# MLA's values of two head groups from seven products of two k-tiles, ahead of the second group's queries

## Chip, cores and metric

The kernel runs on one core of one Trainium2 chip. The time is device microseconds of one execution; before the change the median of three runs is 2367.46 us. One execution was also taken by the profiler, and all rows come from it.

## What is computed

A trunk of two residual layers over 256 positions with a width of 2048, in float32. Layer 0 runs 32 Mamba-2 heads and 16 heads of multi-head latent attention (MLA) behind one input projection, and joins both in one output projection; layer 1 is stick-breaking attention; a SwiGLU network follows each. The change concerns MLA alone:

```python
def mla_mixer(c_q, c_kv, k_rope, q_norm, kv_norm, w_uq, w_ukv, cos, sin):
    q = (rms_norm(c_q, q_norm) @ w_uq).reshape(bsz, seq, MLA_HEADS, MLA_NOPE + MLA_ROPE)
    kv = (rms_norm(c_kv, kv_norm) @ w_ukv).reshape(bsz, seq, MLA_HEADS, MLA_NOPE + MLA_V)
    q_nope, q_pe = jnp.split(q, [MLA_NOPE], axis=-1)
    k_nope, v = jnp.split(kv, [MLA_NOPE], axis=-1)
    ...
        s = (jnp.einsum('bqhd,bkhd->bhqk', q_nope[:, q0:q1], k_nope[:, :q1])
             + jnp.einsum('bqhr,bkr->bhqk', q_pe[:, q0:q1], k_pe[:, :q1])).astype(jnp.float32) * scale
        ...
        outs.append(jnp.einsum('bhqk,bkhd->bqhd', p.astype(v.dtype), v[:, :q1]))
```

The values v of a head are 128 columns of `w_ukv` times the 512 normalised latent columns of c_kv: four k-tiles of 128 rows, for two token tiles of 128.

## The kernel before

**Split products.** Every float32 operand is split in a high part, made by a cast on ACT (`split`, L346), and a low part, the difference, made by a subtract on DVE (L352). A product of one k-tile is three matmuls: high by high, low by high, high by low. The low part of a weight overwrites its raw tile.

**Weights.** SP loads weights into six raw slots of 128x2048, in the order in which the code asks for them and as slots come free. High parts lie in four buffers in this stage. A copy that frees a PSUM bank is marked `urgent`; `after_urgent` lets a weight's cast be issued only behind the urgent copies of four weights earlier.

**PSUM.** Four accumulator banks, taken in rotation from `self.banks` by `acc`. Score blocks, transposes and P.V products use another pool.

**Order.** PE's order is that of the code. ACT, DVE, SP and POOL each run one queue in an order set when the program is built, by priorities: weights first in the order of their use, urgent work ahead of it.

**The MLA stage** (`mla_group`, L1464) handles four groups of four heads, one after the other:

- the rope part of the queries, `project` with 256 columns (matmuls L460, L462, L463), copied by ACT (L1502), turned by POOL;
- the queries without rope and the keys, `project_T` (L508 and L510, copy L517);
- the values, `project` with 512 columns: 4 k-tiles x 2 token tiles x 3 = 24 matmuls, copied out by ACT (L407);
- four heads, spawned at the end of the group as tasks (`mla_head`, L1516) that wake 2, 6, 10 and 14 ticks later, and so run among the next group's projections: a score block on PE (L1526 to L1528), its row maximum on DVE (L1533, L1534), the exp on ACT in two halves (L1536), the normalising on DVE (L1538, L1540); seven ticks later three transposes (L1544) and a copy (L1546), four ticks later the product with the values (L1550, L1551).

Behind group 3 comes the output projection (`project_residual`, in the order `LATE`). It makes two blocks of 512 columns at a time from seven products (`pair`, matmuls L794) whose weight operands are sums made on DVE (L741), and whose data operands are sums too (L691, L701). ACT copies a product out of its bank where it is needed twice (L815), and DVE adds it to another (a "take", L643). The first such pair starts with the products M1 and M5. The heads of group 3 run inside it.

Of the kernel before, what the change touches and what calls it, by code (L numbers as in the profile page):

```python
# [47 lines left out]
class Trunk:  # L48
# [526 lines left out]
    def more_sums(self, st):  # L575

        sub = lambda o, p, q: self.nc.vector.tensor_tensor(o, p, q, op=ALU.subtract)
        add = lambda o, p, q: self.nc.vector.tensor_tensor(o, p, q, op=ALU.add)
        yield 40
        self.join(st["xT"][2][0])  # L580
        a = {}
        for j, (hi, lo) in enumerate(st["xT"][2][1]):
            r = self.s2([2, S])
            add(r, hi.bitcast(F32), lo.bitcast(F32))
            a.update({(t, j): r[:, :, t * P:(t + 1) * P] for t in range(2)})
        yield 1
        s12, s34 = self.s2([4, P]), self.s2([4, P])
        s1, s2, s3, s4 = s12[:, :2], s12[:, 2:], s34[:, :2], s34[:, 2:]
        add(s1, a[1, 0], a[1, 1])
        sub(s2, s1, a[0, 0])  # L590
        sub(s3, a[0, 0], a[1, 0])
        sub(s4, a[0, 1], s2)
        for s in (s12, s34):
            yield 1
            hi, lo = self.s2([4, P], F32R), self.s2([4, P], F32R)
            self.split(hi, lo, s)
            st["N"].append((hi, lo))

    def norm_operand(self, st, j, g):
# [567 lines left out]
    def even(self, st):  # L1167
        nc, i = self.nc, self.i
        win = i["w_in"][0]
        xT = self.pairs(st["xT"], True)  # L1170
        xdt = [[self.spare[2 * n + t] for t in range(2)] for n in range(4)]
        y = [[self.s2([512]) for _ in range(2)] for _ in range(4)]
        conv, ssd = {}, []
        for n in (4, 5, 0, 1, 2, 3):
            ps = self.project(xT, self.cols(win, OFF_XBC + n * 512, first=n == 4), KD)
# [3 lines left out]
            raw = self.evac(ps, AF.Copy, rstd, self.twins)  # L1179
# [8 lines left out]
        cT = []  # L1188
        for off, g in ((OFF_CQ, self.g_q), (OFF_CKV, self.g_kv)):
            ps = self.project(xT, self.cols(win, off), KD)  # L1190
            raw = self.evac(ps, AF.Copy, rstd, self.twins)
            ssq = self.small([P, 2], "ssqc")
            with self.urgent():
# [3 lines left out]
                r = self.rstd(ssq, 512)  # L1197
# [7 lines left out]
        for n in range(4):  # L1205
            ps = self.project(xT, self.cols(win, OFF_Z + n * 512), KD)
# [6 lines left out]
            src, g = lambda t, k: self.twins[t].words[:, k * P:(k + 1) * P], self.g_ssd[:, 4 * n:4 * n + 4]  # L1213
# [24 lines left out]
        self.slots["wh"] += self.more_high  # L1238
        self.project_residual(uT, lambda n: self.cols(wo, n * 512), scale)
        oT = self.operand()  # L1240
        for g in range(4):
            self.mla_group(g, self.pairs(cT[:1]), self.pairs(cT[1:]), oT)
        st = self.norm_begin()
        self.project_residual(oT, lambda n: self.cols(wo, n * 512, r0=SSD_W), None,
                              lambda n: self.norm_next(st, n, self.g_ffn[0]), ("M5", "M3"), self.LATE)
# [218 lines left out]
    def mla_group(self, g, cq, ckv, oT):  # L1464
# [5 lines left out]
        def heads(wd, c0, n):  # L1470
            def view(w, k0, k1):
                for k in range(k0, k1):
                    yield (w[:, k - k0, :4 * n].rearrange("p (h c) -> p h c", c=n),
                           wd[:, k, h0:h0 + 4, c0:c0 + n])
            return view

        qp = self.evac_rope(self.project(cq, heads(wuq, 128, 64), 4, 256), self.twins[g % 2])
# [127 lines left out]
```

## Time and profile before

| | |
|---|---|
| median of the runs | 2367.46 us (2367.45 to 2368.05) |
| the profiled execution, its own time | 2367.47 us |
| its span | 2365.8 us |
| granted TensorE clock, mean | 0.999 |
| group 0's values and group 1 | 415.78 to 448.95 us |
| group 2 | 448.95 to 479.27 us |
| group 3 | 479.27 to 509.60 us |
| first products of the output projection | from 509.60 us |

The span runs from the first to the last instruction; 1.7 us of the execution lie around it. A row of the timeline gives the start of an instruction, its length, engine, line and operation, the tiles written and read with their shapes, and in brackets the idle time ahead of it with what ended it. "x4" joins several like instructions. Lengths of neighbours on an engine overlap a little, so the step from start to start is the cost of one in a row. A matmul's length is far longer than that step, because several are in flight.

### The profile page before, as it was taken

The page shows a single profiled execution, that of the slowest core. Times are in us where ns is not written, and L with a number is a line of the kernel's source. Part 1 is how long each engine was busy: PE and PEld are TensorE (multiplying, and loading weights), DVE is VectorE, ACT ScalarE, POOL GpSimd, SP SyncE. Part 2 cuts the span into 40 slices and gives each one's busy share as a digit, 9 for nine tenths or more (in the row PEclk, how much of TensorE's full clock was granted, in tenths as well). Part 3 has the DMA queues.
Part 4 walks back from the last instruction along what each step waited for, and adds up shares of the span by engine and source line. Part 5 has one row for each costly group of instructions (what it writes and reads, how often), then busy time and mean ns, then how long its engine had stood idle before and what let it go on. Part 6 is the DMA issues. An engine that isn't in the chain of part 4 may idle for free.

```text
span 2365.8 us, 28204 instructions
## 1 busy us (share of the span) xinstructions
PE 2350.3 (99%) x11088; PEld 1955.3 (83%) x11088; DVE 1986.8 (84%) x1639; ACT 1461.5 (62%) x1478; POOL 213.1 (9%) x273
## 2 busy tenths in 40 slices
PE   9999999999999999999999999999999999999998
PEld 7888888988888888888888888888888888888886
DVE  6776587589998889989887898889997988899884
ACT  6655565566665655566655786776665666555663
POOL 1342001110000000000000020110000000000011
PEclk9999999999999999999999999999999999999999
DMA  8655556445666767776776655556657777777773
GB/s 274 205 194 177 184 196 189 133 142 195 230 204 206 226 217 216 221 221 220 219 238 210 202 183 176 186 174 239 229 200 212 222 223 224 216 215 226 218 252 109
DMA packets 271428, 486.33 MB, mean 206 GB/s; under 512 B 22268, under 2 KB 47488, under 8 KB 271296
## 3 DMA queue, kind: packets, MB, share of 16 engines
q1 hardware_dynamic: 255200, 445.95, 57.4%
q0 software_dynamic: 15232, 37.01, 6.4%
q8 instruction: 87, 1.43, 0.2%
q10 hardware_dynamic: 864, 1.57, 0.2%
q14 instruction: 45, 0.37, 0.0%
HBM read 459.24 MB, written 25.20 MB: 205 GB/s over the span
## 4 chain that ended last, share of the span: by engine, by line
PE 95%; DVE 2%; ACT 2%; issue 1%; DMA 0%; SPq 0%; ACTq 0%; DVEq 0%
PE acc L794 54%; PE acc L460 11%; PE acc L463 11%; PE acc L462 11%; PE tr L357 1%; PE acc L508 1%; ACT wh L346 1%; PE at L1455 1%; PE acc L510 0%; DVE wsum L741 0%; DVE wsum L352 0%; DVE w L352 0%; PE at L1526 0%; DMA xres<-in_x_dram 0%; PE at L1527 0%
## 5 line engine op out<-in xcount | busy, mean ns | idle before, releaser
L352 DVE TENSOR_TENSOR w<-w,wh 128x2048 fp32r<-128x2048 f32 (+2 forms) x399 | 892.9, 2245 | 189.7 <-ACT wh L346 183.1
L794 PE MATMUL acc<-wh,s 128*128 128x512 f32 x3896 | 985.4, 391 | 1.5 <-ACT s L815 1.2
L346 ACT CAST wh<-w 128x2048 fp32r<-128x2048 f32 (+2 forms) x399 | 744.7, 1874 | 340.3 <-PE acc L463 147.0
L794 PEld LDWEIGHTS acc<-wh,s 128*128 128x128 f32 x3896 | 725.5, 188 | 150.9 <-ACT s L815 1.7
L460 PE MATMUL acc<-wh,s 128*128 128x512 f32 (+1 forms) x1216 | 482.0, 396 | 0.1
L463 PE MATMUL acc<-wh,s 128*128 128x512 f32 (+1 forms) x1216 | 471.0, 387 | 0.1
L462 PE MATMUL acc<-w,s 128*128 128x512 f32 (+1 forms) x1152 | 445.4, 387 | 0.0
L794 PE MATMUL acc<-w,s 128*128 128x512 f32 x1312 | 355.6, 389 | 0.2 <-DVE w L352 0.2
L794 PEld LDWEIGHTS acc<-w,s 128*128 128x128 f32 x1312 | 246.2, 188 | 52.1 <-DVE w L352 0.6
L463 PEld LDWEIGHTS acc<-wh,s 128*128 128x128 f32 x1216 | 228.3, 188 | 47.9 <-DVE s L381 0.6
L460 PEld LDWEIGHTS acc<-wh,s 128*128 128x128 f32 x1216 | 228.5, 188 | 45.3 <-issue 1.7
L462 PEld LDWEIGHTS acc<-w,s 128*128 128x128 f32 x1152 | 216.7, 188 | 41.8 <-issue 1.4
L352 DVE TENSOR_TENSOR wsum<-wsum,wh 128x2048 fp32r<-128x2048 f32 (+1 forms) x101 | 217.8, 2156 | 3.7 <-ACT wh L346 3.7
L346 ACT CAST wh<-wsum 128x2048 fp32r<-128x2048 f32 (+1 forms) x101 | 182.9, 1811 | 53.9 <-PE acc L794 35.7
L956 POOL DMA_DIRECT2D saved<-s x64 | 55.9, 995 | 1107.1 <-ACT s L955 1106.0
L346 ACT CAST wh<-lent 128x2048 fp32r<-128x2048 f32 (+1 forms) x62 | 114.6, 1859 | 62.0 <-DMA lent<-in_w_gate_dram 19.9
L352 DVE TENSOR_TENSOR lent<-lent,wh 128x2048 fp32r<-128x2048 f32 (+1 forms) x62 | 137.1, 2216 | 11.6 <-ACT wh L346 11.2
L741 DVE TENSOR_TENSOR wsum<-w,wsum 128x2048 f32<-128x2048 f32 (+1 forms) x52 | 104.2, 2004 | 17.8 <-PE acc L794 15.9
L794 PE MATMUL acc<-wsum,s 128*128 128x512 f32 x380 | 104.6, 390 | 1.4 <-DVE wsum L352 1.4
L794 PEld LDWEIGHTS acc<-wsum,s 128*128 128x128 f32 x380 | 71.2, 188 | 17.1 <-DVE wsum L352 2.2
L815 ACT COPY s<-acc 128x512 f32<-128x512 f32 x88 | 51.6, 588 | 39.1 <-PE acc L794 39.1
L741 DVE TENSOR_TENSOR wsum<-w,w 128x2048 f32<-128x2048 f32 (+1 forms) x35 | 71.3, 2038 | 1.7 <-DMA w<-in_w_qkv_dram 1.7
(268 smaller groups left out, 1888.8 us busy)
## 6 DMA issues: line engine op xcount, KB each, us to landing
w<-in_w_down_dram SPq DMA_DIRECT2D x80, 1024.0 KB, 5.0
w<-in_w_gate_dram SPq DMA_DIRECT2D x76, 1024.0 KB, 5.1
w<-in_w_up_dram SPq DMA_DIRECT2D x76, 1024.0 KB, 5.1
w<-in_w_qkv_dram SPq DMA_DIRECT2D x48, 1024.0 KB, 5.0
w<-in_w_in_dram SPq DMA_DIRECT2D x45, 1024.0 KB, 5.2
w<-in_w_out_even_dram SPq DMA_DIRECT2D x32, 1024.0 KB, 5.0
saved<-s POOLq DMA_DIRECT2D x64, 256.0 KB, 7.2
w<-in_w_out_odd_dram SPq DMA_DIRECT2D x16, 1024.0 KB, 4.9
```

The lines of the kernel that those rows point to most:

```text
L346: cast = nc.scalar.copy(hi, src).ins
L352: return nc.vector.tensor_tensor(lo, src, hi.bitcast(F32), op=ALU.subtract).ins
L357: self.nc.tensor.transpose(out.bitcast(F32R), src, self.ident_r)
L460: nc.tensor.matmul(ps[t], hi[:, ts], wh, start=k == 0, stop=False)
L462: slot.used(nc.tensor.matmul(ps[t], hi[:, ts], wl, start=False, stop=False), self.clock)
L463: nc.tensor.matmul(ps[t], lo[:, ts], wh, start=False, stop=k == nk - 1)
L508: nc.tensor.matmul(ps[:, h % 2], wh[:, hs], x, start=k == n == 0, stop=False)
L741: ins = self.nc.vector.tensor_tensor(half(o, so), half(p, sp), half(q, sq), op=ALU.subtract).ins
L794: m = nc.tensor.matmul(ps[b], x, y, start=b not in started, stop=stop, skip_group_check=True)
L815: copied = nc.scalar.copy(o, ps[b]).ins
L956: nc.gpsimd.dma_start(self.saved[n][:, t], s, accum_op=ALU.add)
L1455: nc.tensor.matmul(py[:, ds], rows[c, h // 4][:, h % 4], xdt[c][:, ds], start=True, stop=True)
```

## The change

The values of groups g-1 and g, for g = 1 and 3, are made together by a new function `quad`, ahead of group g's queries; groups 0 and 2 have no value projection of their own. The 512 latent columns are taken as two halves of two k-tiles, the two token tiles and the two groups of heads likewise as halves, so that the product is one of 2x2 blocks by 2x2 blocks, made with seven products M1 to M7 in place of eight. Each product is 2 k-tiles x 3 = 6 matmuls of 128x512 (L641 after the change): 42 for two groups.

The products are issued in the order M1, M2, M5, M6, M3, M7, M4. M1, M6 and M7 go into the bank z, M5 and M3 into p3, M2 into p2, M4 into p4. M1, M5, M6 and M7 are copied out by ACT (L661) and four takes on DVE (L1593) add them to what ends in the banks; these are the values. Afterwards the banks stand in the order p2, p4, z, p3. The four weight sums t1 to t4 are half-width subtracts and adds on DVE; two raw slots hold loaded weights (c0, c1), two the sums (n2, n3). The data sums of the four products that need them (`quad_sums`) are made once, in a task that is spawned ahead of the first group, and serve both quads. The products wait for weights and banks as before; the tasks of heads run among them at the ticks.

```diff
+    def quad_sums(self, st, block, wait):
...
+        yield wait
+        self.join(block[0])
+        a = {}
+        for j, (hi, lo) in enumerate(block[1]):
+            r = self.s2([2, S])
+            add(r, hi.bitcast(F32), lo.bitcast(F32))
...
+        add(s1, a[1, 0], a[1, 1])
+        sub(s2, s1, a[0, 0])
+        sub(s3, a[0, 0], a[1, 0])
+        sub(s4, a[0, 1], s2)
+        for s in (s12, s34):
+            yield 1
+            hi, lo = self.s2([4, P], F32R), self.s2([4, P], F32R)
+            self.split(hi, lo, s)
+            st["N"].append((hi, lo))
+
+    ONLY = ("t1", "t2", "t4", "n0", "n2", "t3", "n1", "n3")
+
+    def quad(self, st, va, vb, left, right, nk=4, order=ONLY, tag="wsum"):
...
+        for m, v in (("c0", va), ("c1", vb)):
+            raw[m] = self.wload(v, 0)
+        self.join(st["quad"])
+        names = ("z", "p3", "p2", "p4")
+        z, p3, p2, p4 = self.banks
+        self.banks = [p2, p4, z, p3]
...
+            if keep:
+                with self.urgent():
+                    kept[keep] = self.s2([512])
+                    nc.scalar.copy(kept[keep], ps[b])
+            with self.urgent():
+                for c, q, take, t in (("p2", "M1", left, 0), ("p4", "M7", left, 1), ("z", "M5", right, 1),
+                                      ("p3", "M6", right, 0)):
+                    if todo[c] == 0 and q in kept:
+                        todo[c] = -1
+                        take(t, ps[c], kept[q])
+
+        bank = {"M1": "z", "M6": "z", "M7": "z", "M5": "p3", "M3": "p3", "M2": "p2", "M4": "p4"}
...
+            if m == "t1":
+                src["n2"] = self.wtile(tag)
+                self.wsub(src["n2"], raw["c1"], raw["c0"], 0, 0, 0)
...
+            elif m == "n0":
+                halves(self.wsplit(raw["c0"], 4, 4, sync), (0, "M1"), (1, "M2"))
+            elif m == "n2":
+                halves(self.wsplit(src["n2"], 4, 4, sync), (0, "M5"), (1, "M6"))
+            elif m == "n1":
+                halves(self.wsplit(raw["c1"], 4), (1, "M3"), (0, "M7"))
+            elif m == "n3":
+                halves(self.wsplit(src["n3"], 2, 2), (0, "M4"))
...
+        kv = {"xT": cT[1:], "N": []}
+        kv["quad"] = self.spawn(self.quad_sums(kv, cT[1], 4))
         for g in range(4):
-            self.mla_group(g, self.pairs(cT[:1]), self.pairs(cT[1:]), oT)
+            self.mla_group(g, self.pairs(cT[:1]), self.pairs(cT[1:]), kv, oT)
...
+        if g % 2 == 0:
+            self.v = [[None, None], [None, None]]
+        else:
+            def take(n):
+                def sum_up(t, c, s):
+                    nc.vector.tensor_tensor(s, c, s, op=ALU.add)
+                    self.v[n][t] = s
+                return sum_up
+            self.quad(kv, heads(wkv, 128, 128, -4), heads(wkv, 128, 128), take(0), take(1), tag="w")
+        v = self.v[g % 2]
         qp = self.evac_rope(self.project(cq, heads(wuq, 128, 64), 4, 256), self.twins[g % 2])
         q = self.project_T(cq, heads(wuq, 0, 128))
         k = self.project_T(ckv, heads(wkv, 0, 128))
-        v = self.evac(self.project(ckv, heads(wkv, 128, 128), 4))
```

The diff moves instructions on engines whose order it does not write out. The first place is ACT between group 0's keys and group 1's rope queries. Names are tile names with buffer numbers: `s2` data tiles, `wh` high parts, `w4` to `w9` raw slots, `acc` accumulators, `at` scores, `mx` and `sm` a head's maximum and sum. Before:

```order
L346 CAST wh0_65<-w8_78 128x2048
L407 COPY s2_310_3273<-acc_308_3241 128x512
L407 COPY s2_311_3275<-acc_309_3242 128x512
L346 CAST wh1_66<-w4_70 128x2048
L346 CAST wh2_67<-w5_72 128x4x256
L1536 ACT_TABLE_LOAD
L1536 ACTIVATE s2_319_3308,sm_318_3307<-at_316_3299,mx_317_3306 128x128
L1536 ACTIVATE s2_319_3308,sm_318_3307<-at_316_3299,mx_317_3306 128x256
L1502 COPY s2_320_3329<-acc_314_3279 128x256
```

The same place after the change, where `acc_318` is the bank z, `acc_319` p3, and the copies L661 are, in turn, those of M1, M5, M6 and M7:

```order
L346 CAST wh0_65<-w8_78 128x1024
L661 COPY s2_322_3284<-acc_318_3269 128x512
L346 CAST wh1_66<-w4_70 128x4x256
L1656 ACT_TABLE_LOAD
L1656 ACTIVATE s2_326_3301,sm_325_3300<-at_323_3292,mx_324_3299 128x128
L661 COPY s2_327_3319<-acc_319_3270 128x512
L661 COPY s2_328_3327<-acc_318_3269 128x512
L1656 ACTIVATE s2_326_3301,sm_325_3300<-at_323_3292,mx_324_3299 128x256
L346 CAST wh2_67<-w5_72 128x2048
L1656 ACTIVATE s2_332_3354,sm_331_3353<-at_329_3345,mx_330_3352 128x128
L661 COPY s2_333_3363<-acc_318_3269 128x512
```

Two evacuations that stood ahead of the first head's exp are gone; copies of M5 and M6 now stand between its two halves, and that of M7 between those of the second head.

The second place is DVE ahead of the output projection's first pair. `wsum` and some `w` tiles take the weight sums. Before, from the first of the sums on:

```order
L741 TENSOR_TENSOR wsum10_82<-w9_80,w7_76 128x2048
L1534 TENSOR_SCALAR mx_409_3948<-mx_409_3948 128x2
L352 TENSOR_TENSOR w7_75<-w7_76,wh2_67 128x2048
L1538 RECIPROCAL sm_410_3949<-sm_410_3949 128x2
L1540 TENSOR_SCALAR s2_411_3950<-s2_411_3950,sm_410_3949 128x128
L1540 TENSOR_SCALAR s2_411_3950<-s2_411_3950,sm_410_3949 128x256
L741 TENSOR_TENSOR wsum11_84<-w8_78,wsum10_82 128x2048
```

After the change, from the second quad's last two takes (M7's and M4's) to the same sum and the second one:

```order
L1593 TENSOR_TENSOR s2_416_3956<-acc_400_3877,s2_416_3956 128x512
L1593 TENSOR_TENSOR s2_425_4011<-acc_403_3880,s2_425_4011 128x512
L1658 RECIPROCAL sm_423_4001<-sm_423_4001 128x2
L1660 TENSOR_SCALAR s2_424_4002<-s2_424_4002,sm_423_4001 128x128
L1660 TENSOR_SCALAR s2_424_4002<-s2_424_4002,sm_423_4001 128x256
L850 TENSOR_TENSOR wsum10_82<-w5_72,w6_74 128x2048
L352 TENSOR_TENSOR w4_69<-w4_70,wh1_66 128x2048
L1653 TENSOR_REDUCE mx_434_4073<-at_433_4066 128x1 x2
L352 TENSOR_TENSOR w6_73<-w6_74,wh2_67 128x2048
L1654 TENSOR_SCALAR mx_434_4073<-mx_434_4073 128x2
L850 TENSOR_TENSOR wsum11_84<-w9_80,wsum10_82 128x2048
```

The first weight sum of the projection stood behind group 2's values on PE and now stands behind the takes of a quad; the low part of group 3's keys (`w4`) stands behind it.

More of the change, by code (lines that the diff above doesn't have):

```diff
@@ L597, in more_sums @@
             st["N"].append((hi, lo))
+    def quad_sums(self, st, block, wait):
+        sub = lambda o, p, q: self.nc.vector.tensor_tensor(o, p, q, op=ALU.subtract)
+        add = lambda o, p, q: self.nc.vector.tensor_tensor(o, p, q, op=ALU.add)
+        yield wait
[4 more added lines that the diff above has]
+            add(r, hi.bitcast(F32), lo.bitcast(F32))
+            a.update({(t, j): r[:, :, t * P:(t + 1) * P] for t in range(2)})
+        yield 1
+        s12, s34 = self.s2([4, P]), self.s2([4, P])
+        s1, s2, s3, s4 = s12[:, :2], s12[:, 2:], s34[:, :2], s34[:, 2:]
+        add(s1, a[1, 0], a[1, 1])
[3 more added lines that the diff above has]
+        for s in (s12, s34):
+            yield 1
+            hi, lo = self.s2([4, P], F32R), self.s2([4, P], F32R)
+            self.split(hi, lo, s)
+            st["N"].append((hi, lo))
@@ new lines, with mm, add, ops @@
+    ONLY = ("t1", "t2", "t4", "n0", "n2", "t3", "n1", "n3")
+    def quad(self, st, va, vb, left, right, nk=4, order=ONLY, tag="wsum"):
+        nc, raw, src = self.nc, {}, {}
+        for m, v in (("c0", va), ("c1", vb)):
[4 more added lines that the diff above has]
+        self.banks = [p2, p4, z, p3]
+        ps = {n: self.pacc.tile([P, 512], F32, name=self.nm("acc"), tag=b, bufs=1)
+              for n, b in zip(names, (z, p3, p2, p4))}
+        more = nk // 4 - 1
+        todo = {"z": 3 + more, "p3": 2 + more, "p2": 1 + more, "p4": 1 + more}
+        started, kept = set(), {}
+        def mm(b, x, y, stop=False):
+            m = nc.tensor.matmul(ps[b], x, y, start=b not in started, stop=stop, skip_group_check=True)
+            started.add(b)
+            return m
+        def add(b, x, w, keep=None):
+            wh, wl, slot = w
+            n = len(x)
+            for k, (hi, lo) in enumerate(x):
+                mm(b, hi, wh[:, k])
+                mm(b, lo, wh[:, k])
+                if k == 1 and n > 2:
+                    self.tick()
+            for k, (hi, lo) in enumerate(x):
+                self.clock += 1
+                slot.used(mm(b, hi, wl[:, k], stop=k == n - 1), self.clock)
+            self.tick()
+            todo[b] -= 1
+            if keep:
[9 more added lines that the diff above has]
+        bank = {"M1": "z", "M6": "z", "M7": "z", "M5": "p3", "M3": "p3", "M2": "p2", "M4": "p4"}
+        def ops(m):
+            if m in ("M1", "M2", "M4"):
+                return [self.operand_tile(st, k + 2 * (m != "M1"), m == "M4") for k in range(2)]
+            n = (5, 6, 7, 3).index(int(m[1]))
+            return [tuple(o[:, n % 2 * 2 + k] for o in st["N"][n // 2]) for k in range(2)]
+        def halves(w, *ms):
+            wh, wl, slot = w
+            for n, m in ms:
+                at = slice(2 * n, 2 * n + 2)
+                add(bank[m], ops(m), (wh[:, at], wl[:, at], slot), m if m in ("M1", "M5", "M6", "M7") else None)
+        sync = mybir.DependencyClass.Sync
+        for m in order:
+            if m == "t1":
+                src["n2"] = self.wtile(tag)
+                self.wsub(src["n2"], raw["c1"], raw["c0"], 0, 0, 0)
+            elif m == "t2":
+                self.wsub(src["n2"], raw["c1"], src["n2"], 1, 1, 0)
+            elif m == "t3":
+                self.wsub(raw["c1"], raw["c1"], raw["c1"], 0, 1, 0)
+            elif m == "t4":
+                src["n3"] = self.wtile(tag)
+                self.wsub(src["n3"], raw["c0"], src["n2"], 0, 1, 1)
+            elif m == "n0":
[7 more added lines that the diff above has]
+            else:
+                k0 = 4 * int(m[1])
+                w = self.wsplit(self.wload(va if m[0] == "a" else vb, k0), 8)
+                for t, b in enumerate(("p2", "p4")) if m[0] == "a" else ((1, "z"), (0, "p3")):
+                    add(b, [self.operand_tile(st, k0 + k, t) for k in range(4)], w)
@@ L1462, in ssd_group, with mla_group @@
         nc.gpsimd.tensor_tensor(y[1], y[1], yo, op=ALU.add)
-    def mla_group(self, g, cq, ckv, oT):
+    def mla_group(self, g, cq, ckv, kv, oT):
         nc, i = self.nc, self.i
@@ L1468, in mla_group, with heads @@
         h0 = 4 * g
-        def heads(wd, c0, n):
+        def heads(wd, c0, n, more=0):
             def view(w, k0, k1):
@@ L1473, in view @@
                     yield (w[:, k - k0, :4 * n].rearrange("p (h c) -> p h c", c=n),
-                           wd[:, k, h0:h0 + 4, c0:c0 + n])
+                           wd[:, k, h0 + more:h0 + more + 4, c0:c0 + n])
             return view
+        if g % 2 == 0:
+            self.v = [[None, None], [None, None]]
+        else:
+            def take(n):
[5 more added lines that the diff above has]
+        v = self.v[g % 2]
         qp = self.evac_rope(self.project(cq, heads(wuq, 128, 64), 4, 256), self.twins[g % 2])
```

## The prediction, made before the changed kernel ran

> **What bounds the kernel now.** I read the page first: the busy times with their share of the span, and the chain that ended last.
>
> ```profile
> PE 2350.3 (99%) x11088; PEld 1955.3 (83%) x11088; DVE 1986.8 (84%) x1639; ACT 1461.5 (62%) x1478; POOL 213.1 (9%) x273
> ...
> PE 95%; DVE 2%; ACT 2%; issue 1%; DMA 0%; SPq 0%; ACTq 0%; DVEq 0%
> ```
>
> PE is busy 99% of the span and carries 95% of the chain. A whole-run share says nothing of one stage, so I cut the MLA stage by windows: group 0's values with group 1, then group 2, group 3, and the start of the output projection. The columns are the window and its length, then the busy time and count of PE, of its weight loads, of DVE, ACT and POOL, the granted clock, the DMA share and GB/s.
>
> ```profile
> 415.78:448.95 33.17, 33.17 (x224) 30.30 (x223) 17.54 (x30) 19.32 (x36) 5.36 (x12) 1.00 0.49 128
> 448.95:479.27 30.32, 30.32 (x217) 28.24 (x216) 15.12 (x30) 16.93 (x41) 5.13 (x12) 1.00 0.47 139
> 479.27:509.60 30.33, 30.33 (x218) 28.24 (x217) 24.83 (x35) 17.06 (x37) 10.45 (x12) 1.00 0.41 139
> 509.60:560.00 50.40, 49.16 (x246) 41.06 (x245) 41.53 (x56) 33.76 (x55) 0.00 (x0) 1.00 0.43 146
> ```
>
> PE has no idle time in the groups, so there a matmul less is time saved, and a wait of PE is time lost. DVE is half idle in groups 1 and 2 and fuller (24.83 of 30.33) in group 3, where the output projection is prepared. The only wait is 50.40 - 49.16 = 1.24 behind 509.60.
>
> **The saving.** The first two rows are the first and the last of group 0's 24 value matmuls, the third the first of the next rope queries.
>
> ```profile
> 415.78 0.40 PE L460 MATMUL acc<-wh,s 128*128 128x512 f32 x1
> ...
> 421.02 0.39 PE L463 MATMUL acc<-wh,s 128*128 128x512 f32 x1
> 421.25 0.28 PE L460 MATMUL acc<-wh,s 128*128 128x256 f32 x1
> ```
>
> 24 matmuls in 421.25 - 415.78 = 5.47 us: 0.228 each. Two groups take 48 before and 42 after, so both pairs of groups save 12 x 0.228 = 2.74 us. One product of six is 1.36.
>
> [...]
>
> **What the quad waits for: four banks, two of them used again.** M5 goes into the bank p3 and M3 into it again, after ACT has copied M5 out; the same holds for M1, M6 and M7 in z. ACT works in its written order, and there the copy of M5 stands behind an exp of a head whose scores PE has just made, and that exp behind DVE's maximum. The prices:
>
> ```profile
> 422.68 0.39 PE L1526 MATMUL at<-s,s 128*128 128x128 f32 x2
> ...
> 424.13 0.36 PE L460 MATMUL acc<-wh,s 128*128 128x256 f32 x1
> ```
>
> A score block between two projection matmuls is 424.13 - 422.68 = 1.45. On ACT:
>
> ```profile
> 415.98 0.59 ACT L517 COPY s<-acc 128x512 f32<-128x512 f32 x1 [2.65 <-PE acc L510]
> ...
> 426.91 1.28 ACT L1536 ACT_TABLE_LOAD   x1
> 428.21 0.37 ACT L1536 ACTIVATE s<-at,mx 128x128 f32<-128x128 f32 x1
> 428.47 0.19 ACT L1536 ACTIVATION_READ_ACCUMULATOR s<-at,mx 128x1 f32 x1
> 428.57 0.47 ACT L1536 ACTIVATE s<-at,mx 128x256 f32<-128x256 f32 x1
> ...
> 433.62 1.91 ACT L346 CAST wh<-w 128x2048 fp32r<-128x2048 f32 x1
> ```
>
> The first row began 0.20 after the matmul that it waited for (415.78, where the keys end): the handoff from PE to a reader. The first half of an exp takes 0.36 (428.21 to 428.57). On DVE:
>
> ```profile
> 387.63 0.69 DVE L643 TENSOR_TENSOR s<-acc,s 128x512 f32<-128x512 f32 x1
> ...
> 423.87 2.29 DVE L352 TENSOR_TENSOR w<-w,wh 128x2048 fp32r<-128x2048 f32 x1 [3.16 <-DMA w<-in_w_uq_dram]
> 426.07 0.61 DVE L1533 TENSOR_REDUCE mx<-at 128x1 f32<-128x128 f32 x2
> 426.72 0.17 DVE L1534 TENSOR_SCALAR mx<-mx 128x2 f32<-128x2 f32 x1
> 426.93 1.22 DVE L352 TENSOR_TENSOR w<-w,wh 128x1024 fp32r<-128x1024 f32 x1
> ```
>
> Followers start about 0.09 before the end shown (423.87 + 2.29 against 426.07), so 2.20 for a full low part; two reduces are 0.65 to the next start.
>
> *A, first quad, M3.* From the end of M2: handoff 0.20, take 0.69, n3's low part 1.22, reduces 0.65, the rope queries' low part 1.22, maximum 0.17: 4.15, less about 0.15 of overlaps, 4.0. Then the table load 1.28, the exp 0.36, the copy of M5 0.59: 6.2. PE's cover is the score block 1.45 and M5 and M6 at 1.36: 4.2. Wait **2.0**. Behind M3 on PE stand M7 and head 1's scores, so all of it is lost. If the load does not wait for the maximum but runs early, A is 0.7.
>
> [...]
>
> *D, second quad to the next rope queries.* The banks are left as p2, p4, z, p3, so the next rope queries take p2 and, three 256-column matmuls later (0.12 each, an estimate as half the 0.228 for half the width, together 0.36), p4, which M4, the last product, has just filled. It comes free with DVE's take of M4, which stands behind M7's, which needs M7's copy, behind head 2's exp, behind its maximum. From the end of that score block: 0.20 + 0.65 + 0.17 = 1.02, exp 0.36, copy 0.59, two takes 1.29, in all 3.26, and 0.06 to restart. PE has M4 1.36 and 0.36. Wait **1.6**.
>
> *B, the same place in the first quad.* The reduces stand behind the queries' low part (2.29), this behind its cast (1.91), the cast behind the exp that A delays: DVE reaches the reduces about 0.6 later. Wait **2.2**.
>
> *C, second quad, M3.* Here a second score block lies ahead of M6: 1.02 + 0.36 + 0.59 + 0.06 = 2.03 against M6's 1.36. Wait **0.6**.
>
> Each such wait is seen once today, at the output projection's third product:
>
> ```profile
> 516.71 1.07 PE L794 MATMUL acc<-wsum,s 128*128 128x512 f32 x4
> ...
> 517.86 1.10 ACT L815 COPY s<-acc 128x512 f32<-128x512 f32 x2
> ...
> 519.02 1.20 PE L794 MATMUL acc<-wh,s 128*128 128x512 f32 x4 [1.24 <-ACT s L815]
> ```
>
> PE restarts 0.06 after the copy, and the first four matmuls take 0.13 longer (1.20, 1.07): that surcharge I add per wait. This wait stays; with its products' preparation shifted I walk it at 0.9, so -0.3.
>
> **What the quad takes from the output projection (E).** Before, group 3's values lay ahead of the first pair as cover.
>
> ```profile
> 484.63 2.28 DVE L741 TENSOR_TENSOR wsum<-w,w 128x2048 f32<-128x2048 f32 x1
> ...
> 504.47 0.69 DVE L352 TENSOR_TENSOR s<-s,s 128x512 fp32r<-128x512 f32 x1 [0.31 <-ACT s L346]
> ...
> 509.60 1.07 PE L794 MATMUL acc<-wh,s 128*128 128x512 f32 x4
> ```
>
> The pair's first operand's low part was ready at 505.16 and wanted at 509.60: 4.4 us of slack; the first weight sum ran from 484.63. Now 5.47 of values are gone from group 3's stretch, and two of its four score blocks: 30.33 - 5.47 - 2 x 1.45 = 22.0, with D's 1.6 about 23.5 from M4's end to the pair. DVE, from the last take (1.9 after M4's end), has seven full-width operations, 7 x 2.20 = 15.4, and some 21 small ones (reduces, maxima, normalising, four operand sums at 0.69), 7.2, then the operand's low part 0.69: 25.2. Wait **1.7**, between 1.0 (small ones overlap) and 2.2 (an operation waits for its cast).
>
> **At nothing.** The operand sums (2 x 0.69, four half ones, two splits: about 4.3 of DVE, 1.2 of ACT) run in group 0's queries and keys, ahead of 415.78, as do the first quad's weight sums (four half-width ones): if DVE is late there, n2 starts late, 1 us for 1 us. The four copies replace four evacuations on ACT. The quad's weights lie in four of the six raw slots. A load takes
>
> ```profile
> w<-in_w_out_even_dram SPq DMA_DIRECT2D x32, 1024.0 KB, 5.0
> ```
>
> 5.0 us to land, and SP issues in the order in which slots come free, as before. The tightest is the second operand of the first weight sum: its slot is free at M7's end, a score block and M4 (1.45 + 1.36 = 2.8) ahead of M4's end, so it lands 2.2 behind it, just when DVE comes to it. POOL's rope work, 5.13 to 5.36 busy in a group of 30, isn't moved.
>
> **Sum.** 2.0 + 2.2 + 0.6 + 1.6 + 1.7 = 8.1; five surcharges 0.65; -0.3; saving -2.74: +5.7. The profiled execution took 2367.47, the median of the runs shown is 2367.46, so both give 2367.47 + 5.7 = **2373.2 us**, 0.24% slower. About 0.2%, 4.7 us, is what a measurement can tell from no change: 2362.7 to 2372.2.
>
> **Rivals.** *The cover at the pair suffices* (not slower): DVE's seven full-width operations end early, because the weight sums and low parts find the idle half of group 2's DVE time, 30.32 - 15.12, ahead of M4's end. For: loads may land early, and the small operations overlap. Against: they are ordered behind the takes. It decides where DVE's load after the last take falls under 21.6 (23.5 - 1.9, operand included) instead of 23.3. E and its surcharge go: 2373.2 - 1.8 = 2371.4. Chance 0.25.
>
> *All waits hide*: the copies are not late, since PE lags behind what my walk gives it or DVE's chain is shorter. Only the saving stands: 2364.7. For: no wait at PE in any group today. Against: A to D start at an event of PE itself (the end of M2 or of a block), so no lead of the other engines helps. Waits together must fall under 2.7 to be faster at all. Chance 0.12.
>
> *Weights late*: the six slots are held longer, and the tightest load above lands after DVE wants it, and every microsecond is added to E. A whole landing would be 5.0; I take 3: 2376.2. For: 4 of 6 slots for a block of 10 us. Against: DMA share 0.4 to 0.5. Chance 0.15.
>
> *The clock swings*: two quads of 42 x 0.228 = 9.6 us at half speed would give +19, 2392. Against: 1.00 in every row here, the one with the wait too. Chance 0.02. [...] That the change fails to do what it says is excluded by the order of PE's instructions: 42 where 48 were.
>
> **Chances.** The forecast, all five waits, 0.46, spreads over 2371 to 2375.5, four fifths of it above 2372.2: 0.37. With the late weights and the clock, 0.54 slower. No change: 0.09 of the forecast, the 0.25 of the pair's rival and about 0.09 of the hidden waits: 0.43. Faster by over 0.2% needs more than the whole saving: 0.03. Range: the low end is the four block waits at their lower ends (A 0.7, the others less by a third) without E, 2367.5; the high end the weights' rival with 0.8 more in E and A, 2377.0. It leaves out most of the hidden waits, the clock and a tail.
>
> **What would show it.** Right: PE waits of 2.0 and 0.6 at the quads' M3 ended by ACT's copy, of 2.2 and 1.6 at the rope queries' second bank ended by DVE's take, and one ahead of the first pair ended by DVE's low part of an operand; the stage's windows longer by the waits less 2.74. Wrong: a quad without idle time, a wait ended by a DMA, or a clock under 1.00.

## The result and the profile after

The changed kernel takes 2380.76 us (median of six runs, 2377.28 to 2381.4) where the kernel before takes 2367.64 (six runs, 2367.45 to 2368.05): a ratio of 1.0054 with a 95% interval of 1.0044 to 1.0064, so 13 us or 0.54% slower. The forecast was 2373.2 with a range up to 2377.0: the direction was right and the size was not.

The page after, the same two lines as before (busy times, and the chain that ended last); its span is 2379.0 us, its own time 2380.7:

```profile
PE 2352.0 (99%) x11076; PEld 1955.2 (82%) x11076; DVE 2015.8 (85%) x1667; ACT 1468.4 (62%) x1484; POOL 225.0 (9%) x273
...
PE 92%; issue 4%; DVE 2%; ACT 1%; POOL 1%; DMA 0%; SPq 0%; ACTq 0%; DVEq 0%; POOLq 0%
```

PE issues 12 instructions less and is yet busy 1.7 us longer, and POOL, which nobody asked to do more, is busy 12 us longer (213.1 before). Both are hints at the two things that the forecast missed. What PE waits for in the stage, from 380 to 560 us (line waited at, releaser, sum, times, longest):

```profile
PE tr L357 <- POOL twin L1470: 5.1, 2, 3.5
PE acc L460 <- DVE s L1593: 3.3, 2, 1.9
PE acc L641 <- ACT s L661: 2.3, 2, 1.7
PE acc L903 <- ACT s L924: 0.7, 1, 0.7
PE acc L903 <- DVE s L352: 0.5, 1, 0.5
```

The second to the fifth row are the forecast's B and D, A and C, the old wait, and E. The first, the costliest, is in no term of its sum. In the timeline, both waits for POOL and those of the first quad:

```profile
417.65 0.53 PE L357 MATMUL tr<-ident_r,twinwords 128*128 128x128 f32 x4 [3.48 <-POOL twin L1470]
...
430.01 1.20 PE L641 MATMUL acc<-wh,s 128*128 128x512 f32 x4 [1.74 <-ACT s L661]
...
438.18 0.39 PE L460 MATMUL acc<-wh,s 128*128 128x256 f32 x1 [1.86 <-DVE s L1593]
...
521.37 0.54 PE L357 MATMUL tr<-ident_r,twinwords 128*128 128x128 f32 x4 [1.66 <-POOL twin L1470]
```

The second quad's waits at the same places are 0.54 and 1.49, E is 0.48 and the old one 0.68. All eight sum to 11.9 where there was one of 1.24: 10.7 more. The same stretch by windows, cut at the first waits (the column before the DMA share is the granted clock):

```profile
414.17:417.65 3.48, 0.01 (x2) 0.00 (x1) 2.58 (x4) 2.90 (x5) 3.35 (x5) 1.00 0.02 3
418.50:421.70 3.20, 3.20 (x15) 3.02 (x14) 2.60 (x2) 0.79 (x2) 0.00 (x0) 0.54 0.00 0
436.32:438.18 1.86, 0.00 (x1) 0.00 (x1) 1.35 (x3) 1.86 (x5) 0.00 (x0) 1.00 0.92 246
438.30:441.50 3.20, 3.20 (x17) 3.20 (x18) 2.89 (x4) 2.18 (x3) 0.00 (x0) 0.54 1.09 321
```

In the second and the fourth row, behind two of the waits, PE works with no idle time at half the clock. Cut finer, each stretch is 3.41 us long (418.05 to 421.46, 438.53 to 441.94) and loses half of it, together 3.4. That is why the busy time grew with less work in it.

Put together: 10.7 of waits, 3.4 of half clock and seven restarts more at about 0.13 (0.9), less 2.74 saved, are 12.3. From the start of group 0's rope queries to the output projection's third product PE took 117.99 us before (401.03 to 519.02) and takes 131.85 now (401.06 to 532.91), 13.9 more. So 1.6 of the stage's loss is in no term: its matmuls follow each other a little less closely, and the cause is not shown. The rest of the kernel is 0.7 shorter, and the spans differ by 13.2.

Why is POOL late for the wait of 3.48? Its rope work in group 0, in the changed kernel (start and length):

```profile
404.23 0.98 POOL L1464 TENSOR_TENSOR ropea<-s,rope 128x128 f32<-128x128 f32 x1 [83.46 <-ACT s L1622]
405.17 1.44 POOL L1465 TENSOR_TENSOR ropeb<-s,rope 128x128 f32<-128x128 f32 x1
...
408.57 2.50 POOL L1469 TENSOR_TENSOR ropeb<-s,rope 128x128 f32<-128x128 f32 x1
411.03 2.51 POOL L1464 TENSOR_TENSOR ropea<-s,rope 128x128 f32<-128x128 f32 x1
...
417.14 0.46 POOL L1470 TENSOR_TENSOR twin<-ropea,ropeb 128x128 f32<-128x128 f32 x1
```

and DVE beside it:

```profile
408.21 5.00 DVE L352 TENSOR_TENSOR w<-w,wh 128x2048 fp32r<-128x2048 f32 x2
```

The two operations of 2.50 and 2.51 lie in step with DVE's two subtracts, 5.00 together. All twelve took from 404.23 to 417.60, 13.4 us, and PE's transposes start 0.05 later. The profile of before had the sign of it, and the forecast did not look there:

```profile
404.19 1.04 POOL L1353 TENSOR_TENSOR ropea<-s,rope 128x128 f32<-128x128 f32 x1 [83.48 <-ACT s L1502]
405.19 1.53 POOL L1354 TENSOR_TENSOR ropeb<-s,rope 128x128 f32<-128x128 f32 x1
406.69 0.46 POOL L1357 TENSOR_TENSOR ropea<-s,rope 128x128 f32<-128x128 f32 x1
```

The first multiply takes 1.04 beside the end of a subtract of DVE (402.62 to 404.90), the second 1.53 beside another (405.18 to 406.40), and the third, of the same shape, 0.46 once DVE is idle. In group 3 of the same profile the full price stood, on POOL and on DVE beside it:

```profile
490.34 2.50 POOL L1355 TENSOR_TENSOR twin<-ropea,ropeb 128x128 f32<-128x128 f32 x1
489.99 2.54 DVE L741 TENSOR_TENSOR wsum<-w,wsum 128x2048 f32<-128x2048 f32 x1
```

There the rope took 10.6 us already before the change (488.54 to 499.15), and PE came for it at 499.75, just late enough not to wait.

### The profile page after: what moved, and what is told of

Same layout as the page of the kernel before. It is cut to its first block, busy times and chain, and to the rows that moved or that the text cites. A ratio compares the mean times of both kernels' runs of the same rounds, so it can differ in the third digit from the quotient of the medians.

```text
span 2379.0 us, 28225 instructions
## 1 busy us (share of the span) xinstructions
PE 2352.0 (99%) x11076; PEld 1955.2 (82%) x11076; DVE 2015.8 (85%) x1667; ACT 1468.4 (62%) x1484; POOL 225.0 (9%) x273
## 4 chain that ended last, share of the span: by engine, by line
PE 92%; issue 4%; DVE 2%; ACT 1%; POOL 1%; DMA 0%; SPq 0%; ACTq 0%; DVEq 0%; POOLq 0%
PE acc L903 52%; PE acc L460 11%; PE acc L463 11%; PE acc L462 11%; PE tr L357 1%; PE acc L508 1%; PE at L1566 1%; DVE w L352 0%; PE acc L641 0%; ACT wh L346 0%; DVE wsum L850 0%; PE acc L510 0%; PE at L1646 0%; PE at L1647 0%; DMA xres<-in_x_dram 0%
## 5 line engine op out<-in xcount | busy, mean ns | idle before, releaser
L460 PE MATMUL acc<-wh,s 128*128 128x512 f32 (+1 forms) x1184 | 469.8, 397 | 3.5 <-DVE s L1593 3.3
L463 PE MATMUL acc<-wh,s 128*128 128x512 f32 (+1 forms) x1184 | 459.1, 388 | 0.1
L462 PE MATMUL acc<-w,s 128*128 128x512 f32 (+1 forms) x1120 | 433.4, 387 | 0.0
L903 PEld LDWEIGHTS acc<-w,s 128*128 128x128 f32 x1312 | 246.2, 188 | 52.1 <-DVE w L352 0.6
L462 PEld LDWEIGHTS acc<-w,s 128*128 128x128 f32 x1120 | 211.1, 189 | 41.0 <-issue 1.4
L850 DVE TENSOR_TENSOR w<-w,w 128x2048 f32<-128x2048 f32 (+1 forms) x35 | 74.1, 2117 | 0.9 <-PE acc L510 0.8
```

The costliest lines, as they stand in the source:

```text
L460: nc.tensor.matmul(ps[t], hi[:, ts], wh, start=k == 0, stop=False)
L462: slot.used(nc.tensor.matmul(ps[t], hi[:, ts], wl, start=False, stop=False), self.clock)
L463: nc.tensor.matmul(ps[t], lo[:, ts], wh, start=False, stop=k == nk - 1)
L850: ins = self.nc.vector.tensor_tensor(half(o, so), half(p, sp), half(q, sq), op=ALU.subtract).ins
L903: m = nc.tensor.matmul(ps[b], x, y, start=b not in started, stop=stop, skip_group_check=True)
```

## The experiments

The theory after reading: the five block waits are as walked; besides them DVE's new work (weight sums, operand sums) slows POOL's rope until PE waits for it, and PE's waits are followed by half clock. The rivals: POOL is slow for another reason; the clock falls for another reason, such as the load of the quad; the place ahead of group 1's queries is at fault and not the seven products. Times are medians; the kernel before took 2367.51 to 2367.56 beside these runs.

**1. Another order of banks.**

```diff
-        self.banks = [p2, p4, z, p3]
+        self.banks = [p2, p3, z, p4]
```

> The change with one line altered: after a quad the banks stand in the order p2, p3, z, p4, so the next rope queries take p2 and p3 and not the bank of the last product. Theory (each wait costs its length, and two waits close together also cost clock): the waits of 1.86 and 1.49 us at the rope queries' second bank go, with two restart surcharges of 0.13, and the stretch of half clock behind 438 us, some 3.5 us long and so about 1.75 us of loss, goes too, since only the 1.74 at M3 is left there: 3.35 + 0.26 + 1.75 = 5.4 less, about 2375.4 us. Rival (the clock does not follow from these waits): only 3.6 less, 2377.2, with half clock still near 440 us. Second rival (the wait moves on to the queries' bank z): nothing gained, 2380.8.

It took 2378.56 us (2376.92 to 2379.3). No wait for a take is left, so B and D are what they were said to be. But less was won than the theory asked: the waits of 3.48 and 1.74 stay, and the timeline of PE has the rope wait of group 3 at 3.38 in place of 1.66, with half clock behind it.

```profile
518.64 0.54 PE L357 MATMUL tr<-ident_r,twinwords 128*128 128x128 f32 x4 [3.38 <-POOL twin L1470]
```

PE reached the transposes earlier and POOL did not come earlier: the wait moved. The clock near 440 us was full, as the theory has it. But at the end of the wait of 3.48 and behind it, it was half for twice as long as in the changed kernel, 6.83 us in place of 3.41:

```profile
416.79:420.21 3.42, 2.76 (x14) 2.76 (x15) 1.97 (x2) 1.46 (x1) 0.53 (x2) 0.50 0.00 0
420.21:423.62 3.41, 3.41 (x11) 2.79 (x10) 0.91 (x1) 1.67 (x3) 0.00 (x0) 0.50 0.46 117
```

So this run has as many stretches of half clock as the changed kernel has, and one of them is longer: that, with the moved wait, is where the expected gain went.

**2. The rope transposes later.**

```diff
-            yield 7
+            yield 9
             pt = self.tr([2, S])
```

> The change with the transposes of the turned rope queries two ticks later (9 in place of 7), so that they stand behind M1. Theory (PE waits there because POOL's rope work takes twice as long as before, and the wait can be covered): group 0's wait of 3.48 shrinks to about 0.7, since half a head pair of keys (1.4) and M1 (1.36) now lie ahead of it; group 3's 1.66 goes, but the wait for the output projection's first operand, 0.48, grows by up to 1.2 since it is no longer hidden behind it; the half clock behind 418 us, about 1.75 of loss, goes: 2.8 + 0.5 + 1.75 = about 5 less, 2375.7 us. POOL's operations stay as long as in the changed kernel. Rival (the wait moves to the first score block, which needs these transposes): 1 to 2 less at most, 2379.

2379.76 us (2378.36 to 2381.03): the rival. The rope wait fell to 0.68, but the first score block waited 1.56 for the transposed queries, and ahead of the output projection the first operand was late by 1.95, with half clock behind it. In the profiled execution, the fastest of the four, no half clock follows the first quad's waits, though those at M3 and at the rope queries' bank are 1.46 and 1.88, 8 us apart: two waits close together do not bring it by themselves. Covering the wait did not help here, where the next consumer was close.

**3. DVE's load alone, in the kernel before.**

```diff
+        if twin is self.twins[0] and not hasattr(self, "once"):
+            self.once = x = qp.rearrange("p t h d -> p (t h d)").unsqueeze(1).to_broadcast([P, 4, 512])
+            with self.urgent():
+                for _ in range(4):
+                    nc.vector.tensor_tensor(self.slots["wsum"][1].raw, x, x, op=ALU.subtract)
```

> The kernel before with one thing added: four subtracts of 128x2048 on DVE, urgent, as soon as group 0's rope queries are copied out, into a tile that nobody reads. They stand for the weight sums and operand sums that the change puts there. Theory (POOL and DVE hinder each other): POOL's twelve rope operations, 0.46 us each beside an idle DVE, grow to up to 2.5 beside these, some 10 to 13 us together in place of 6.8; the transposes that waited for nothing before wait 0 to 3 us, and the time lies between 2367.6 and 2371. Rival (POOL was slow in the changed kernel for another reason): POOL stays at 0.46 an operation, 2367.6 us.

2375.7 us (2374.88 to 2377.01), ratio 1.0035 (1.0022 to 1.0047): more than the theory asked. Four subtracts that nobody reads, on an engine that was half idle, cost 8 us. The timeline of POOL's rope:

```profile
405.07 0.45 POOL L1354 TENSOR_TENSOR ropeb<-s,rope 128x128 f32<-128x128 f32 x1
405.49 2.51 POOL L1357 TENSOR_TENSOR ropea<-s,rope 128x128 f32<-128x128 f32 x1
407.96 2.51 POOL L1355 TENSOR_TENSOR twin<-ropea,ropeb 128x128 f32<-128x128 f32 x1
...
418.23 0.45 POOL L1357 TENSOR_TENSOR ropea<-s,rope 128x128 f32<-128x128 f32 x1
```

One operation of POOL per subtract of DVE, 2.38 to 2.51 each, and 0.45 where DVE is idle. PE and the clock in windows:

```profile
414.01:420.08 6.07, 0.00 (x1) 0.00 (x0) 3.53 (x2) 0.00 (x0) 5.94 (x7) 0.67 0.21 64
420.08:426.30 6.22, 6.22 (x23) 5.55 (x24) 2.15 (x3) 2.38 (x2) 0.00 (x0) 0.50 0.23 52
```

6.07 idle, then 6.22 at half clock (3.1 lost): 9.2 of the 9.5 by which the spans differ. With no quad in this kernel, both rivals on POOL and on the clock fall: DVE's load makes POOL late, and idle time of PE brings the half clock.

**4. PE's idle time filled.**

```diff
             yield 7
+            if fill:
+                self.fill(fill, 29)
             pt = self.tr([2, S])
...
+        if g == 1:
+            self.fill(cq(0)[0], 16)
         qp = self.evac_rope(...)
```

> The change with idle time of PE filled by products that nobody reads: 29 matmuls of 128x256 (about 3.5 us) ahead of group 0's rope transposes, and 16 (about 1.9 us) between the first quad and the next rope queries. The waits themselves stay: PE works in them. Theory (the half clock at 418 and at 438 us follows from idle time of PE): both stretches go, each about 3.5 us at half speed, so 1.75 each: about 3.5 less, 2377.2 us, granted clock 0.999 in the mean. Rival (the clock falls for another reason, such as the load of the quad itself): it falls all the same and the time stays at 2380.8.

2376.52 us (2376.14 to 2377.41), 4.2 less than the changed kernel although PE does 5.6 us of useless products (3.68 and 1.92). From 414 to 445 us, where both stretches of half clock lay, the clock is full now. But one stretch came up that the changed kernel did not have, behind group 3's rope wait, in the windows and the timeline:

```profile
414.00:445.00 31.00, 30.23 (x201) 27.08 (x201) 22.46 (x34) 20.59 (x36) 5.11 (x7) 1.00 0.67 187
517.04 0.54 PE L357 MATMUL tr<-ident_r,twinwords 128*128 128x128 f32 x4 [1.66 <-POOL twin L1470]
514.70:518.11 3.41, 1.75 (x16) 1.55 (x15) 3.23 (x7) 3.41 (x7) 2.21 (x4) 1.00 0.00 0
518.11:521.53 3.42, 3.42 (x14) 2.99 (x13) 2.83 (x4) 2.34 (x4) 0.00 (x0) 0.50 0.21 13
```

A wait of 1.66 was followed by half clock here, and a wait of the same 1.66 in the changed kernel was not. The length alone does not decide between them; the last section shows what else may.

**5. Rope on DVE.** The bank order of run 1, and the rope work of groups 0 and 3 on DVE.

```diff
-        tt = nc.gpsimd.tensor_tensor
+        tt = (eng or nc.gpsimd).tensor_tensor
...
-        qp = self.evac_rope(self.project(...), self.twins[g % 2])
+        qp = self.evac_rope(self.project(...), self.twins[g % 2], nc.vector if g in (0, 3) else None)
```

> The changed kernel with the bank order p2, p3, z, p4 of the earlier run, and with the twelve rope operations of groups 0 and 3 on DVE in place of POOL, urgent. Theory (the rope waits come from POOL and DVE hindering each other): the waits for POOL of 3.48 and up to 3.4 us go, as do the half-clock stretches behind 418 and 438 (3.5 us of loss) and the bank waits (3.6 with surcharges). In group 3 DVE gets some 2.4 more to do, and the output projection's first operand, no longer hidden behind the rope wait, is late by about 4. From 2380.8: 3.6 + 3.6 + 1.7 + 3.5 less, 3.5 more: about 2372 us. Rival (DVE is the bound and the rope would be as late on it): a wait of 3 us stays at group 0's rope transposes, now ended by DVE, 2376 us or more.

2377.94 us (2375.21 to 2378.18), well above the 2372 expected. Group 0's rope wait is gone altogether, so it was POOL's. But with that wait gone PE comes to the end of M2 5.1 us earlier (418.74 for 423.82) and DVE does not keep up: its low part ahead of the first maximum starts at 419.98, where one stood at 418.82. So M3's wait, whose chain runs through it, grew from 1.74 to 3.19, with 6.83 us of half clock at its end and behind it; in group 3 the transposes now waited 2.38 for DVE and the first operand 2.06.

**6. One quad only.** Groups 2 and 3 as before; M4 ahead of M3; group 0's rope on DVE.

```diff
-        self.banks = [p2, p4, z, p3]
+        self.banks = [p2, p4, p3, z]
...
-    ONLY = ("t1", "t2", "t4", "n0", "n2", "t3", "n1", "n3")
+    ONLY = ("t1", "t2", "t4", "n0", "n2", "t3", "n3", "n1")
...
+        if g > 1:
+            v = self.evac(self.project(ckv, heads(wkv, 128, 128), 4))
```

> One quad only, for groups 0 and 1; groups 2 and 3 make their values as before. M4 is issued ahead of M3, the banks stand as p2, p4, p3, z after it, and group 0's rope work is on DVE. Theory: groups 2 and 3 are as before (no wait at C, D, E or at group 3's rope), six matmuls less save 1.37, M4 covers M3's wait down to 0.4 to 1.4, and nothing is left for the clock: 2366.5 to 2367.8 us, no measurable difference from the kernel before. Rival (the first quad costs in itself, whatever is covered): waits of 3.5 and 1.8 with half clock remain in the first quad, 2371 us or more.

2374.67 us (2374.47 to 2376.18). The bank order was badly chosen: p4's take needs M7's copy, M7 is now the last product, and the next rope queries asked for p4 second. PE's timeline:

```profile
425.88 1.21 PE L641 MATMUL acc<-wh,s 128*128 128x512 f32 x4 [1.46 <-ACT s L661]
...
435.52 0.48 PE L460 MATMUL acc<-wh,s 128*128 128x256 f32 x1 [4.69 <-DVE s L1593]
```

M3's wait is 1.46 with a whole product more ahead of it, just above the 0.4 to 1.4 expected. The run says nothing on what one quad can give; run 9 does.

**7. The place without the seven products.**

```diff
-            self.quad(kv, heads(wkv, 128, 128, -4), heads(wkv, 128, 128), take(0), take(1), tag="w")
+            for n, more in ((0, -4), (1, 0)):
+                self.v[n][:] = self.evac(self.project(ckv, heads(wkv, 128, 128, more), 4))
```

> The values of both groups at the place of the quad, but by the two ordinary projections of 24 matmuls each, without weight sums, operand sums, keep copies and takes: the move without the seven products. Theory (the added work on DVE, not the place, makes the rope late in group 0): no wait for POOL in group 0, no waits at banks, full clock there; only what the move costs ahead of the output projection is left, where 5.5 us of cover are gone: 0 to 3 us, so 2367.5 to 2370.5. Rival (the place is at fault): most of the 13 us stays, 2375 us or more.

2370.14 us (2369.79 to 2370.76), ratio 1.0011 (1.0002 to 1.0021): inside the theory's span, and the rival falls. The place alone costs 2.6 us, nearly all of it in group 3, as PE's timeline shows:

```profile
510.75 0.53 PE L357 MATMUL tr<-ident_r,twinwords 128*128 128x128 f32 x4 [1.50 <-POOL twin L1469]
...
513.50 0.96 PE L903 MATMUL acc<-wh,s 128*128 128x512 f32 x3 [0.48 <-DVE s L352]
```

POOL is not slower there than before: its rope work takes 9.9 us (500.75 to 510.69) where it took 10.6. It starts later, 12.2 us behind the first matmul of the rope queries (488.57) where it was 9.3 (479.27 to 488.54), since the copy on ACT stands behind an exp that waits for DVE's maximum until 499.49. Group 0 has no wait. So of the 13 us, 2.6 are the place's, and the seven products cost 10.6 net of the 2.74 that they save.

**8. M4 ahead of M3**, on top of run 5.

```diff
-        self.banks = [p2, p3, z, p4]
+        self.banks = [p2, p3, p4, z]
...
-    ONLY = ("t1", "t2", "t4", "n0", "n2", "t3", "n1", "n3")
+    ONLY = ("t1", "t2", "t4", "n0", "n2", "t3", "n3", "n1")
```

> As the run with rope on DVE, and M4 ahead of M3 in both quads (banks p2, p3, p4, z after it). Theory (M3's wait is the copy of M5 behind an exp, and another product covers it): the waits of 1.74 and 0.54 fall to 0 to 0.8 and 0, about 1.5 less than that run, 2370.5 us. Rival (the exp comes later by as much, since DVE has the maximum behind another low part): the same time as that run, 2372.

2372.22 us (2371.25 to 2374.19), 5.7 less than run 5, where 1.5 was expected: M3's wait fell from 3.19 to 1.46 only, but the half clock behind it went too, C is gone, and the waits ahead of the output projection fell from 2.38 and 2.06 to 1.72 and 0.74. These two are left, with 1.46 at M3, 0.55 at the queries' bank and one stretch of half clock behind the 1.72.

**9. One quad with every wait treated.** Run 6 with the bank order of run 8, and group 0's heads woken three ticks later, which puts the copies of M5 and M6 ahead of the first exp on ACT.

```diff
-        tasks = [self.spawn(self.mla_head(h, qp, q, k, v, g, o, 2 + 4 * h, done), self.URGENT) for h in range(4)]
+        tasks = [self.spawn(self.mla_head(h, qp, q, k, v, g, o, (5 if g in (0,) else 2) + 4 * h, done), self.URGENT) for h in range(4)]
```

> One quad only (groups 0 and 1), group 0's rope work on DVE, M4 ahead of M3, the banks left as p2, p3, p4, z (in the earlier run of this kind p4, the bank of the last take, came second by my choice, and cost 4.7), and group 0's heads woken three ticks later, so that the copies of M5 and M6 stand ahead of the first exp on ACT. Theory (every wait of the quad has one of the causes named: POOL beside DVE, the bank order, a copy behind an exp): no wait of PE over 0.5 in the quad, full clock, and the six saved matmuls remain: 2367.5 - 1.4 = 2366.1, up to 2367 us with restarts. Rival (something else in the quad costs, or the later heads bring a wait of their own): 2368 us or more.

2367.55 us (2366.99 to 2367.87, eleven runs), ratio 1.0 (0.9991 to 1.0009): no difference from the kernel before. The quad's only wait is 0.35, and in the window from 400 to 430 us the clock is full:

```profile
400.00:430.00 30.00, 29.65 (x201) 27.07 (x200) 27.36 (x38) 18.56 (x22) 0.00 (x0) 1.00 0.55 148
```

So the named causes are all that made PE wait in the first quad, but for this 0.35. The time is neither of the two expected. Of the 1.37 saved only 0.26 are seen at the output projection's third product, which starts at 518.76 where it was 519.02. The stretch from group 0's values to group 2's queries has six matmuls less than before (218 for 224):

```profile
415.82:448.64 32.82, 32.47 (x218) 29.16 (x217) 25.56 (x40) 23.95 (x42) 6.24 (x12) 1.00 0.71 193
```

PE is busy 32.47 in place of 33.17, 0.70 less and not 1.37, and it waits 0.35. So about half of the saving is lost without a wait: the matmuls that stayed follow each other less closely, 0.42 of it at the 256-column ones. Why is not shown.

**10. Both quads with the same**, on top of run 8.

```diff
-        ... self.mla_head(h, qp, q, k, v, g, o, 2 + 4 * h, done) ...
+        ... self.mla_head(h, qp, q, k, v, g, o, (5 if g in (0, 2) else 2) + 4 * h, done) ...
```

> The run with M4 ahead, 2372.2, and the heads of groups 0 and 2 woken three ticks later. Theory: M3's wait of 1.46 and the 0.55 behind it go; what is left is ahead of the output projection, 1.7 at group 3's rope and 0.7 at its first operand, with or without a stretch of half clock (up to 1.75), against 2.74 saved: 2367.5 + 2.4 + 0.3 + 0 to 1.75 - 2.7 - 0.5 = 2367 to 2369 us. Rival (the end of group 3 is hit harder, since the second quad's heads run later too): 2371 us or more.

2372.92 us (2372.15 to 2373.89), ratio 1.0023 (1.0014 to 1.0032): the rival's time. The first quad is as in run 9, but the wait at group 3's rope, 1.72 in run 8, moved on to the output projection's first operand, in PE's timeline:

```profile
511.65 3.32 PE L903 MATMUL acc<-wh,s 128*128 128x512 f32 x7 [2.60 <-DVE s L352]
```

with half clock behind it, and smaller waits follow. That operand came 26.0 us behind the start of group 3's rope queries (485.61), where it was 26.4 in run 8 (488.75 to 515.17): DVE's work up to it takes about as long as in run 8, and PE is there earlier. That the later heads crowd it, as the rival has it, is not shown. None of these runs found a place for the second quad's DVE work that costs nothing.

## Why the prediction was wrong

**A was right in its mechanism and nearly in its size.** The timeline of ACT in the first quad, after the change:

```profile
427.73 1.28 ACT L1656 ACT_TABLE_LOAD   x1 [3.09 <-DVE mx L1654]
429.03 0.37 ACT L1656 ACTIVATE s<-at,mx 128x128 f32<-128x128 f32 x1
429.29 0.19 ACT L1656 ACTIVATION_READ_ACCUMULATOR s<-at,mx 128x1 f32 x1
429.38 1.06 ACT L661 COPY s<-acc 128x512 f32<-128x512 f32 x2
```

and that of DVE:

```profile
424.09 0.69 DVE L1593 TENSOR_TENSOR s<-acc,s 128x512 f32<-128x512 f32 x1 [2.99 <-PE acc L641]
424.69 1.22 DVE L352 TENSOR_TENSOR w<-w,wh 128x1024 fp32r<-128x1024 f32 x1
425.83 0.62 DVE L1653 TENSOR_REDUCE mx<-at 128x1 f32<-128x128 f32 x2
426.36 1.22 DVE L352 TENSOR_TENSOR w<-w,wh 128x1024 fp32r<-128x1024 f32 x1
427.49 0.16 DVE L1654 TENSOR_SCALAR mx<-mx 128x2 f32<-128x2 f32 x1
```

The load waits for the maximum, as assumed, and the exp starts 0.02 behind it. M3 starts at 430.01, 6.2 us after M2's end at 423.82 (the start of the score block): the 6.2 of the walk. PE's cover was 4.45 and not 4.2, so the wait is 1.74 and not 2.0. From the start of the load to that of the exp it is 1.30, here and before.

**B, C, D** were 2.2, 0.6 and 1.6 and measured 1.86, 0.54 and 1.49. Run 1 shows that the bank order made B and D. C's own terms give 0.67, so it was 0.1 low as added up. The restarts and the saving are priced from rows of before; no run measures the restarts, and in run 9 half of the saving is not seen.

**E** was 1.7 and measured 0.48, as its cause would have it once another wait stands ahead of it: DVE went on while PE waited 1.66 for POOL. Where that wait was covered, in run 2, E was 1.95. The old wait went from 1.24 to 0.68, 0.6 less where 0.3 was forecast.

**The step that failed** is the list "At nothing": "POOL's rope work, 5.13 to 5.36 busy in a group of 30, isn't moved." The reading leaves out the third row of the forecast's own windows, where POOL is busy 10.45 in group 3, beside a DVE that is busy 24.83. In group 0 the rope is not moved, and the work put beside it doubles its length: 13.4 us in place of 7.0, and a wait of 3.48. In group 3 it was long already, and it now starts 11.2 us behind the start of its queries in place of 9.3 and takes 12.2 in place of 10.6: 1.66 of wait. Run 7, without the seven products, has 1.50 there, so most of the second wait comes from the place and not from the products. The two are 5.1. The operand sums and weight sums were costed by DVE's own idle time (it is busy 8.27 of the 15.78 us ahead of 415.78), and nobody asked what else runs beside them; the price stood in the rows of POOL of 1.04, 1.53 and 2.50 where their neighbours have 0.46. For group 0, runs 3 (the load without the quad) and 5 (the rope without POOL) show the cause from both sides; for group 3 it is read from the timelines.

**The second miss** is the clock. The rival had it at 0.02, since the one wait of 1.24 in the profile had left the clock full. A single short wait says nothing about longer ones: behind 3.48 and 1.86 came two stretches at half speed, 3.4 us lost. Run 4 shows that they follow from PE's idle time. The rival's own price of 19 was too high in turn, for the clock fell for 3.4 to 6.8 us behind a wait in the runs with quads and not for a whole quad.

Without these two, 5.1 and 3.4 with their two restarts, the difference of the spans would be 4.4, and the forecast was 5.7. That the two are near is partly luck: E and the other walked waits came out about 2.2 smaller together, and of the 1.6 in no term and the 0.7 gained behind the stage the forecast knew nothing. The low end of the range does not follow from its terms either: 0.7, two thirds of 2.2, 0.6 and 1.6, four restarts of 0.13, -0.3 and -2.74 give 2368.6 and not 2367.5.

The rival on the pair's cover did not come: E waited, if only 0.48, and in run 2 for long. Late weights did not come either: no wait of PE in the stage ends with a DMA. That all waits hide was excluded by the first rows of the profile.

## What to carry to other kernels

Work put on a half idle engine is not free if it slows another engine that runs beside it, as POOL's operations went here from 0.46 to 2.50 us: look in the profile of before for the same operation at two lengths, and see what ran beside the longer one. A product saved on the bounding engine must be set against every new point where that engine waits, and each wait against the clock behind it, which was half for 3.41 us or more behind several waits of 1.66 us and more here. A block that needs copies out of its own banks wants them ahead of any work that waits for another engine, and the next user of the banks should take first those that were released first.

## What the runs showed of the hardware that was not expected

**POOL and DVE.** A POOL operation of 128x128 took 0.45 to 0.46 beside an idle DVE and mostly 2.50 or 2.51 beside DVE's subtracts of 128x2048: in run 3 one POOL operation for each of DVE's. DVE paid little: 2.43 to 2.54 each in place of the 2.29 shown before. Beside DVE's operations of 0.68 POOL took 0.63 or 0.64 in places. Why the two hinder each other is not shown.

**The clock.** In the kept traces every stretch of half clock in this stage is 3.41 us long or two or three times that: 6.83 in runs 1 and 5, 10.24 in run 3, where it began within the wait of 6.07. The starts within one run lie whole multiples of 3.413 apart: 418.05 and 438.53 in the changed kernel (6 of them), 416.79 and 519.19 in run 1 (30), 425.77 and 521.34 in run 5 (28). So the clock behaves as if it were set on a grid of time, and a wait counts by what of it falls into one window. In the changed kernel, cut on its grid:

```profile
428.29:431.70 3.41, 1.69 (x7) 1.42 (x8) 0.71 (x3) 3.40 (x8) 0.00 (x0) 1.00 0.97 245
435.11:438.53 3.42, 1.56 (x10) 1.22 (x9) 2.29 (x8) 2.66 (x6) 0.00 (x0) 1.00 1.03 281
517.03:520.45 3.42, 2.68 (x22) 2.42 (x20) 3.38 (x9) 2.80 (x7) 3.42 (x5) 1.00 0.59 229
520.45:523.86 3.41, 2.27 (x17) 1.95 (x17) 3.27 (x4) 2.98 (x6) 0.79 (x2) 1.00 0.00 0
```

The wait of 1.86 lies whole in the second window, and half clock follows. That of 1.66 is split between the third and the fourth, and nothing follows; in run 4 a wait of the same 1.66 lay whole in one window (514.70 to 518.11), and half clock followed. In the nine kernels whose traces show the grid, every window ahead of a stretch had 1.66 us or more without work on PE, and a window at full clock with up to 1.51 was never followed by one. A window at half clock was followed by another where it had 0.56 to 0.66 us without work (runs 1, 3 and 5), or no work at all (run 3), and not where it had 0.28 or less. The first row, with 1.72, was not followed by one either, so the border lies between 1.51 and 1.72 us of the 3.41 and is not sharp here. The six runs of the changed kernel spread over 4.1 us where those of before spread over 0.6; that the clock makes this spread is likely and not shown.
